# A hybrid attention layer: transfers of the dilated group on POOL's queue, a zero in SBUF for the first scans, and a set order on ACT and DVE at the start

## The chip, the cores and the metric

The kernel runs on one core of a Trainium2 chip. The engines are named as the profile names them: PE is TensorE (matmuls), DVE is VectorE, ACT is ScalarE, POOL is GpSimd, and SP is SyncE, which here only issues transfers (DMAs). Each engine takes its own instructions in order. SBUF is the on-chip memory, PSUM the banks into which PE writes. The metric is the time of one execution in microseconds (us).

## The reference

One layer of a decoder over x of 1024 tokens x 1024 channels, in float32. Eight heads of 64 use a dilated sliding window (group A), eight use stick-breaking attention (group B), and a gated feed-forward layer of 2816 follows:

```python
h = _rmsnorm(x, attn_norm_w[l])
proj = jnp.einsum('bsd,de->bse', h, w_in[l])          # qa ka va | qs ks vs, 512 columns each
qa = _apply_rope(_rmsnorm(heads(qa, 8), q_norm_w[l]), cos, sin)   # ka likewise
o_dil = _dilated_attention(qa, ka, heads(va, 8))      # branches merged by their denominators
o_sb = _stick_breaking(heads(qs, 8), heads(ksb, 8), heads(vs, 8))
mixed = concat(_rmsnorm(merge(o_dil), ...), _rmsnorm(merge(o_sb), ...))
x = x + mixed @ w_out[l]
h = _rmsnorm(x, ffn_norm_w[l])
x = x + (silu(h @ w_gate[l]) * (h @ w_up[l])) @ w_down[l]

# stick-breaking: beta[t,s] = sigmoid(q.k/8), for s < t
# A[t,s] = beta[t,s] * prod_{s<j<t} (1 - beta[t,j]);  o = A v
# dilated: branches with (window, dilation) (128,1), (512,4), (2048,16)
```

## The kernel before

**Numbers.** Every float32 operand is held as a high and a low part, and a product is three matmuls (lines 91, 94, 95). The high part is a copy on ACT, the low part a subtraction on DVE or POOL; for the tokens that is `split` (lines 61 and 62: hh and hl).

**Stages.** From 0 to about 75 us the eight token blocks of 128 are normed, turned over by PE (`norm_t`: xn on DVE at line 103, ptr at line 109, then `split`), and multiplied by the weights of group A's V (va). Then come the projections of K and Q, from about 165 us the dilated attention of four pairs of heads, from about 350 us the stick-breaking attention of four pairs, and then the output projection and the feed-forward layer. Projections of later pairs run in the background of the attention.

**What sets the order.** The kernel is written in the Tile framework. A scheduler orders each engine's instructions by a simulated time; tiles of one tag share a number of buffers, and `after(i, first, why)` tells the scheduler to put `i` behind `first` without a wait. All transfers are issued on SP's queue, in the order of the scheduler, and a transfer that waits for its data or its buffer holds those behind it.

**The start.** `tok_weights` (line 135) loads the weights of V in eight pieces (raw), makes the high part wt on ACT (line 146), and the low part wt on DVE for even pieces, on POOL for odd ones (line 147). `norm1` takes a token block's square on ACT (line 162); POOL makes the root of it (lines 56 and 57, rs).

**The dilated group.** For each half of a pair, `factors` writes row maxima and sums to memory (sums<-st, line 440, two transfers), reads them in another layout (x<-sums, line 442), weighs them on DVE and ACT (the first step is low<-x, line 448), writes the weights (fac<-fe, line 461) and reads them spread over the partitions (fac<-fac, line 466, two transfers). `finish` multiplies the branches by these on POOL (o, lines 594 and 595) and writes the sum to memory (oa<-o, line 596).

**The stick-breaking group.** K and Q of a pair come back from memory in pieces (rl<-raw, lines 288 and 291, three buffers); kh, kl, qs are their parts (lines 345, 346, 319, 320). For a block of 128 queries, PE computes scores (sc, lines 410 to 413), ACT takes two sigmoids, kp and pb (line 531), DVE a running product from the right over kp (line 534), and POOL (first head) or DVE (second head) multiplies pb by it (line 535). PE turns pb over (pt, line 551), ACT copies it (th), and PE multiplies by V (line 560). The scan's other operand is a column of zeros, which lies in a PSUM bank named aside; its tag "t" is also that of the dilated group's accumulator, so the bank is free when the last output of that group has been copied out:

```python
if aside[0] is None:                                   # attend_b, ahead of its first block
    aside[0] = PS.tile([128, 512], F32, "t", "aside")
    nc.vector.memset(aside[0][:, 0:1], 0.0)
```

Of the kernel before, what the change touches and what calls it, by code (L numbers as in the profile page):

```python
# [24 lines left out]
D = 1024  # L25
# [7 lines left out]
def f(ap):  # L33
    return ap.bitcast(F32)
# [3 lines left out]
def tile_hybrid_block(ctx, tc, x, attn_norm_w, w_in, q_norm_w, k_norm_w, dil_w, sb_w,  # L38
# [12 lines left out]
    mhalf = big.tile([128, 16], F32, name="mhalf")  # L51
    nc.vector.memset(mhalf, -0.5)
    def rstd_of(ss, n, pool, w):

        r = pool.tile([128, 16], F32, tag="rs", name="rs", bufs=6)
        nc.gpsimd.tensor_scalar(r[:, :w], ss, 1.0 / n, EPS, op0=ALU.mult, op1=ALU.add)
        nc.gpsimd.tensor_tensor(r[:, :w], r[:, :w], mhalf[:, :w], op=ALU.pow)
        return r

    def split(h, l, src):  # L60
        nc.scalar.activation(h, src, AF.Copy)  # L61
        nc.vector.tensor_tensor(l, src, f(h), op=ALU.subtract)  # L62

# [33 lines left out]
    def norm_t(xt, ss, wb, tb, dst, work, psum, tag, ptags, parts=1):  # L97

        r = rstd_of(ss, D, big, 1)
        xn = work(tag, "xn")  # L100
        for o in range(0, D, D // parts):
            cc = slice(o, o + D // parts)
            nc.vector.scalar_tensor_tensor(xn[:, cc], xt[:, cc], r[:, 0:1], wb[:, cc], op0=ALU.mult, op1=ALU.mult)
        hf, c = tb // 4, slice((tb % 4) * 128, (tb % 4) * 128 + 128)
        for g in range(2):
            pt = psum.tile([128, 512], F32, ptags[g], "ptr")
            for k in range(4):
                d = 4 * g + k
                nc.tensor.transpose(pt[:, k * 128:(k + 1) * 128], xn[:, d * 128:(d + 1) * 128], ident)
            pt = pt.rearrange("p (k t) -> p k t", k=4)  # L110
            for h, l, ks in dst(g, hf):
                if l is None:
                    if g:
                        nc.scalar.activation(h[:, :, c], pt[:, ks], AF.Copy)
                    else:
                        nc.vector.tensor_copy(h[:, :, c], pt[:, ks])
                else:
                    split(h[:, :, c], l[:, :, c], pt[:, ks])

# [16 lines left out]

    def tok_weights(col, tags):

        w = []
        for d in range(ND):  # L140
            if d % 2 == 0:
                w.append([att.tile([128, 2, 512], FR, tag=t, name="wt", bufs={"P": 6, "G": 2}.get(t, 4)) for t in tags[d:d + 2]])
            raw = big.tile([128, 512], F32, tag=("wraw", "wh", "wl")[d % 3], name="raw", bufs=3)
            nc.sync.dma_start(raw, w_in[d * 128:(d + 1) * 128, col:col + 512])
            h, l = (w[d // 2][k][:, d % 2, :] for k in range(2))
            nc.scalar.activation(h, raw, AF.Copy)
            (nc.gpsimd if col != 1024 or d % 2 else nc.vector).tensor_tensor(l, raw, f(h), op=ALU.subtract)
        return w

    for tb in range(NT):  # L150
# [3 lines left out]
        if tb == 0:  # L154
            nw = att.tile([128, D], F32, tag="v", name="nw", bufs=2)
            nc.sync.dma_start(nw, attn_norm_w.partition_broadcast(128))
            wv = tok_weights(1024, ("qs", "kh") * 4)

    def norm1(tb):
        ss = big.tile([128, 1], F32, tag="ss", name="ss", bufs=4)  # L160
        sq = P4("sq", "G")
        nc.scalar.activation(sq, xts[tb], AF.Square, accum_out=ss)
        norm_t(xts[tb], ss, nw, tb, lambda g, hf: [(hT[g][hf][0], hT[g][hf][1], slice(0, 4))], lambda tag, name: att.tile([128, D], F32, tag="kl", name=name, bufs=2), PS, "v", ("t", "pv"), 1 if tb else 2)

# [17 lines left out]
    for _ in range(12):  # L182
        nc.tensor.matmul(p[:, :128], ident, ident, start=True, stop=True)
    for tb in range(NT):
        norm1(tb)
        p = tok(wv, tb, "d")
# [248 lines left out]
    def factors(st):  # L435
# [5 lines left out]
        x = att.tile([128, 4, 2, 2, 2], F32, tag="x", name="x", bufs=2)  # L441
        nc.sync.dma_start(x.rearrange("p t l m s -> p t (l m s)"), sums.rearrange("(p t) l v -> p t (l v)", t=4))
        fac = dram.tile([2, 2, 512], F32, name="fac")
# [19 lines left out]
        def wide():  # L463
            t = P4("fac", "E").rearrange("p (l t) -> p l t", l=2)
            for s in range(2):
                nc.sync.dma_start(t[64 * s:64 * s + 64], fac[:, s].partition_broadcast(64))
            return t
# [58 lines left out]
    def unit_b(pr, s, qb, tag):  # L526
# [6 lines left out]
        rv = kp[:, n - 1::-1] if n == 1024 else kp[:, :n][:, ::-1]  # L533
        nc.vector.tensor_tensor_scan(rv, rv, aside[0][:, 0:1].to_broadcast([128, n]), 1.0, op0=ALU.mult, op1=ALU.bypass)  # L534
        (nc.gpsimd, nc.vector)[s].tensor_tensor(p[:, :n - 1], p[:, :n - 1], kp[:, 1:n], op=ALU.mult)
# [54 lines left out]
    def finish(pr, hf, o, wide):  # L590
# [4 lines left out]
        nc.gpsimd.tensor_tensor(t[0], t[0], t[1], op=ALU.add)  # L595
        nc.sync.dma_start(o[:, 512 * hf:512 * hf + 512], t[0])

# [26 lines left out]
    def attend_b(pr, o):  # L624

        if aside[0] is None:
            aside[0] = PS.tile([128, 512], F32, "t", "aside")
            nc.vector.memset(aside[0][:, 0:1], 0.0)
        late = None
        for g in range(4):  # L630
            pq = []
            for k in range(2):
# [536 lines left out]
```

## Time and profile before

| | |
|---|---|
| time, median of 3 runs | 1310.41 us (1310.36 to 1313.09) |
| profiled execution | 1310.01 us |
| its span | 1308.2 us, 18283 instructions |
| PE busy | 1264.8 us, 97% of the span |
| weight loads (beside PE) | 998.6 us, 76% |
| DVE busy | 839.7 us, 64% |
| ACT busy | 621.4 us, 47% |
| POOL busy | 390.3 us, 30% |
| mean granted clock of PE | 0.99 |
| transfers | all on one queue, 171.42 MB, 42.1% of the 16 DMA engines |

The span reaches from the first to the last instruction in the trace. In a timeline, the number in brackets is how long the engine stood idle before the instruction, with what released it; several like instructions in a row are one line with their count, and then the time is that of all together. SPq is SP's queue, and the time there is the time to issue the transfer, not to land it. The clock is the share of full speed that was granted to PE.

### The profile page before, as it was taken

How to read it: one execution, taken by the hardware profiler on the slowest of the kernel's cores; microseconds unless marked ns; L12 is line 12 of the kernel's file. 1: busy time of each engine (PE TensorE's matmuls, PEld its weight loads, DVE VectorE, ACT ScalarE, POOL GpSimd, SP SyncE). 2: the span in 40 equal slices, each digit the busy share in tenths (PEclk: the TensorE clock that was granted, in tenths of full speed). 3: DMA queues.
4: the chain of work that ended last, by engine and by line, in shares of the span. 5: the costliest groups of instructions: out<-in, count | busy, mean ns of one | idle time of the engine just before them, and what ended most of it. 6: DMA issues, size and time to landing. Idle time of an engine off the chain costs nothing.

```text
span 1308.2 us, 18283 instructions
## 1 busy us (share of the span) xinstructions
PE 1264.8 (97%) x6260; PEld 998.6 (76%) x6260; DVE 839.7 (64%) x1408; ACT 621.4 (47%) x1305; POOL 390.3 (30%) x334
## 2 busy tenths in 40 slices
PE   7999999999879988999999999999999999999998
PEld 6888887776656766767888888888888887788786
DVE  4224346566477768664788676665546878986775
ACT  6331177776587777753565222233333223344443
POOL 6378722422223234243312222221222321100000
PEclk9999999999989999999999999999999999999999
DMA  9533143544513243132236545323456448503642
GB/s 286 209 112 106 57 130 99 132 132 131 137 60 113 65 170 137 42 103 91 73 123 224 169 153 166 103 87 101 133 150 196 127 151 304 165 18 109 197 137 81
DMA packets 189325, 172.59 MB, mean 132 GB/s; under 512 B 33712, under 2 KB 134192, under 8 KB 189232
## 3 DMA queue, kind: packets, MB, share of 16 engines
q1 hardware_dynamic: 189232, 171.42, 42.1%
q8 instruction: 49, 0.80, 0.3%
q14 instruction: 44, 0.36, 0.1%
HBM read 133.96 MB, written 37.42 MB: 131 GB/s over the span
## 4 chain that ended last, share of the span: by engine, by line
PE 87%; DMA 4%; ACT 3%; DVE 3%; issue 2%; SPq 0%; POOL 0%; DVEq 0%; ACTq 0%; POOLq 0%
PE yd L1069 14%; PE gu L94 11%; PE gu L95 11%; PE gu L91 11%; PE va L95 3%; PE va L91 3%; PE va L94 3%; PE pp L91 3%; PE pp L94 3%; PE pp L95 3%; PE pv L560 2%; PE yo L91 2%; PE pv L487 2%; PE yo L95 2%; PE yo L94 2%; PE pt L551 2%
## 5 line engine op out<-in xcount | busy, mean ns | idle before, releaser
L843 ACT ACTIVATE wh<-wr 128x512 fp32r<-128x512 f32 x132 | 83.4, 632 | 209.5 <-PE gu L94 164.2
L94 PE MATMUL gu<-t,wh 128*128 128x512 f32 x352 | 139.0, 395 | 0.0
L91 PE MATMUL gu<-t,wh 128*128 128x512 f32 x352 | 138.9, 395 | 0.0
L95 PE MATMUL gu<-t,wl 128*128 128x512 f32 x352 | 138.9, 394 | 0.0
L1069 PE MATMUL yd<-dl,dh 128*128 128x512 f32 x308 | 122.1, 396 | 3.1 <-DVE dl L844 3.1
L1069 PE MATMUL yd<-dh,dl 128*128 128x512 f32 x308 | 121.2, 393 | 0.0
L94 PE MATMUL gu<-b,wh 128*128 128x512 f32 x264 | 104.5, 396 | 0.0
L91 PE MATMUL gu<-b,wh 128*128 128x512 f32 x264 | 104.4, 396 | 0.0
L95 PE MATMUL gu<-b,wl 128*128 128x512 f32 x264 | 104.2, 396 | 0.0
L534 DVE TENSOR_TENSOR_SCAN kp<-kp,aside 128x128 f32<-128x128 f32 (+7 forms) x64 | 85.4, 1347 | 29.2 <-ACT kp L531 28.9
L844 DVE TENSOR_TENSOR wl<-wr,wh 128x512 fp32r<-128x512 f32 x105 | 80.5, 767 | 7.6 <-ACT wh L843 7.5
L1069 PE MATMUL yd<-dh 128*128 128x512 f32 x308 | 84.6, 395 | 0.0
L91 PE MATMUL va<-wt,hh 128*128 128x512 f32 x192 | 76.6, 405 | 2.9 <-ACT hh L61 2.9
L95 PE MATMUL va<-wt,hl 128*128 128x512 f32 x192 | 76.5, 401 | 1.9 <-DVE hl L62 1.9
L91 PEld LDWEIGHTS gu<-t,wh 128*128 128x128 f32 x352 | 66.2, 188 | 15.7
L94 PEld LDWEIGHTS gu<-t,wh 128*128 128x128 f32 x352 | 66.2, 188 | 15.7
L95 PEld LDWEIGHTS gu<-t,wl 128*128 128x128 f32 x352 | 66.2, 188 | 15.6
L91 PE MATMUL pp<-hh,wh 128*128 128x512 f32 x192 | 77.9, 406 | 0.0
L843 ACT ACTIVATE dh<-wd 128x512 fp32r<-128x512 f32 x55 | 34.8, 632 | 90.0 <-PE yd L1069 82.4
L94 PE MATMUL va<-wt,hh 128*128 128x512 f32 x192 | 76.3, 400 | 0.0
L95 PE MATMUL pp<-hh,wl 128*128 128x512 f32 x192 | 76.0, 396 | 0.0
L94 PE MATMUL pp<-hl,wh 128*128 128x512 f32 x192 | 75.6, 394 | 0.0
(214 smaller groups left out, 3067.7 us busy)
## 6 DMA issues: line engine op xcount, KB each, us to landing
wd<-in_w_down_dram SPq DMA_DIRECT2D x88, 256.0 KB, 2.9
wr<-in_w_gate_dram SPq DMA_DIRECT2D x80, 256.0 KB, 3.0
wr<-in_w_up_dram SPq DMA_DIRECT2D x60, 256.0 KB, 3.1
raw<-in_w_in_dram SPq DMA_DIRECT2D x48, 256.0 KB, 4.2
raw<-in_w_out_dram SPq DMA_DIRECT2D x32, 256.0 KB, 2.9
raw<-rq SPq DMA_DIRECT2D x24, 256.0 KB, 2.7
g<-gu SPq DMA_DIRECT2D x20, 256.0 KB, 5.4
xt<-in_x_dram SPq DMA_DIRECT2D x8, 512.0 KB, 6.9
```

The lines of the kernel that those rows point to most:

```text
L91: i = nc.tensor.matmul(ps, a[0], b[0], start=first, stop=False)
L94: nc.tensor.matmul(ps, a[0], b[1], start=False, stop=False)
L95: return nc.tensor.matmul(ps, a[1], b[0], start=False, stop=last)
L487: nc.tensor.matmul(pr.acc[lay][64 * s:64 * s + 64, cols], v[:, 64 * s:64 * s + 64], th[:, c:c + n], start=first, stop=last)
L534: nc.vector.tensor_tensor_scan(rv, rv, aside[0][:, 0:1].to_broadcast([128, n]), 1.0, op0=ALU.mult, op1=ALU.bypass)
L551: i = nc.tensor.transpose(pt[:, c:c + 128], pq[k][s][:, j * 128:(j + 1) * 128], ident)
L560: i = nc.tensor.matmul(pr.pv[64 * s:64 * s + 64, c - n:c], pr.v[:, j, 64 * s:64 * s + 64], th[:, n * s:n * s + n], start=j == 0, stop=j == ...
L843: nc.scalar.activation(h, r, AF.Copy)
L844: two(n).tensor_tensor(l, r, f(h), op=ALU.subtract)
L1069: mm = nc.tensor.matmul(pp[k], a[x][:, c], b[y], start=not more and j == 0 and x + y == 0, stop=j == HF - 1 and x == 1, skip_group_check=True)
```

## The change

Three things are changed.

1. The order at the start. All eight raw pieces of V's weights are asked for ahead, as before, but their low parts are all made on DVE. `after` sets this order on ACT (k = 0) and on DVE (k = 1): weight pieces 0 and 1, both parts of token block 0, weight pieces 2 to 7. The square of token block 1 is set between pieces 4 and 5, and those of later blocks behind the first high part of the block two before.
2. In the dilated group, x<-sums, fac<-fac (two) and oa<-o are issued on POOL's queue instead of SP's, 32 transfers in all.
3. A column of zeros, `zero`, lies in SBUF from the start. The scans of the first four query blocks of the first stick-breaking pair (128 to 512 columns, two heads) use it; the bank aside is taken only ahead of the fifth block (g == 2).

```diff
+    zero = big.tile([128, 1], F32, name="zero")
+    nc.vector.memset(zero, 0.0)
...
     def split(h, l, src):
-        nc.scalar.activation(h, src, AF.Copy)
-        nc.vector.tensor_tensor(l, src, f(h), op=ALU.subtract)
+        i = nc.scalar.activation(h, src, AF.Copy)
+        return i, nc.vector.tensor_tensor(l, src, f(h), op=ALU.subtract)
...
-    def tok_weights(col, tags):
-
-        w = []
+    def tok_raw(col, d):
+        raw = big.tile([128, 512], F32, tag=("wraw", "wh", "wl")[d % 3], name="raw", bufs=3)
+        nc.sync.dma_start(raw, w_in[d * 128:(d + 1) * 128, col:col + 512])
+        return raw
+
+    def tok_weights(col, tags, raws=None):
+
+        w, parts = [], []
         for d in range(ND):
...
-            raw = big.tile([128, 512], F32, tag=("wraw", "wh", "wl")[d % 3], name="raw", bufs=3)
-            nc.sync.dma_start(raw, w_in[d * 128:(d + 1) * 128, col:col + 512])
+            raw = raws[d] if raws else tok_raw(col, d)
             h, l = (w[d // 2][k][:, d % 2, :] for k in range(2))
-            nc.scalar.activation(h, raw, AF.Copy)
-            (nc.gpsimd if col != 1024 or d % 2 else nc.vector).tensor_tensor(l, raw, f(h), op=ALU.subtract)
-        return w
+            i = nc.scalar.activation(h, raw, AF.Copy)
+            parts.append((i, (nc.vector if raws else nc.gpsimd).tensor_tensor(l, raw, f(h), op=ALU.subtract)))
+        return (w, parts) if raws else w
...
-            wv = tok_weights(1024, ("qs", "kh") * 4)
+            wv, wparts = tok_weights(1024, ("qs", "kh") * 4, [tok_raw(1024, d) for d in range(ND)])
...
+    before = []
     for tb in range(NT):
-        norm1(tb)
+        sq, made = norm1(tb)
+        if tb == 0:
+
+            for k in range(2):
+                after(made[0][k], wparts[1][k], "order of the first products")
+                after(wparts[2][k], made[1][k], "order of the first products")
+                for d in range(3, ND):
+                    after(wparts[d][k], wparts[d - 1][k], "order of the first products")
+        if tb == 1:
+            after(sq, wparts[4][0], "order of the first products")
+            after(wparts[5][0], sq, "order of the first products")
+        if tb > 1:
+            after(sq, before[-2][1][0], "order of the first products")
+        before.append(made)
...
         x = att.tile([128, 4, 2, 2, 2], F32, tag="x", name="x", bufs=2)
-        nc.sync.dma_start(x.rearrange("p t l m s -> p t (l m s)"), sums.rearrange("(p t) l v -> p t (l v)", t=4))
+        nc.gpsimd.dma_start(x.rearrange("p t l m s -> p t (l m s)"), sums.rearrange("(p t) l v -> p t (l v)", t=4))
...
-                nc.sync.dma_start(t[64 * s:64 * s + 64], fac[:, s].partition_broadcast(64))
+                nc.gpsimd.dma_start(t[64 * s:64 * s + 64], fac[:, s].partition_broadcast(64))
...
-        nc.vector.tensor_tensor_scan(rv, rv, aside[0][:, 0:1].to_broadcast([128, n]), 1.0, op0=ALU.mult, op1=ALU.bypass)
+        nc.vector.tensor_tensor_scan(rv, rv, (aside[0] if aside[0] is not None else zero)[:, 0:1].to_broadcast([128, n]), 1.0, op0=ALU.mult, op1=ALU.bypass)
...
-        nc.sync.dma_start(o[:, 512 * hf:512 * hf + 512], t[0])
+        nc.gpsimd.dma_start(o[:, 512 * hf:512 * hf + 512], t[0])
...
     def attend_b(pr, o):
 
-        if aside[0] is None:
-            aside[0] = PS.tile([128, 512], F32, "t", "aside")
-            nc.vector.memset(aside[0][:, 0:1], 0.0)
         late = None
         for g in range(4):
+            if aside[0] is None and g == 2:
+                aside[0] = PS.tile([128, 512], F32, "t", "aside")
+                nc.vector.memset(aside[0][:, 0:1], 0.0)
```

The change moves instructions in the scheduler's order. DVE's order at the start, in the kernel before (wt is a weight's low part, xn a normed token block, of block 0 in two halves, hl the tokens' low parts):

```order
L103 SCALAR_TENSOR_TENSOR xn<-xt,rs,nw 128x512 x2
L147 TENSOR_TENSOR wt<-raw,wt 128x512 x3
L62 TENSOR_TENSOR hl<-ptr,hh 128x4x128 x2
L147 TENSOR_TENSOR wt<-raw,wt 128x512
L103 SCALAR_TENSOR_TENSOR xn<-xt,rs,nw 128x1024 x3
L62 TENSOR_TENSOR hl<-ptr,hh 128x4x128 x2
```

Here three xn stand between the last weight piece on DVE and the next hl. In the changed kernel DVE starts with:

```order
L106 SCALAR_TENSOR_TENSOR xn<-xt,rs,nw 128x512 x2
L155 TENSOR_TENSOR wt<-raw,wt 128x512 x2
L64 TENSOR_TENSOR hl<-ptr,hh 128x4x128 x2
L155 TENSOR_TENSOR wt<-raw,wt 128x512 x4
L106 SCALAR_TENSOR_TENSOR xn<-xt,rs,nw 128x1024
L155 TENSOR_TENSOR wt<-raw,wt 128x512 x2
L106 SCALAR_TENSOR_TENSOR xn<-xt,rs,nw 128x1024
L64 TENSOR_TENSOR hl<-ptr,hh 128x4x128 x2
```

The low parts of block 0 stand behind two weight pieces instead of three, all eight pieces are in the list, and ahead of the next hl there is one xn less, with two weight pieces between.

SP's order at the passage to the stick-breaking group, before (o<-oa and nw belong to later stages; rl 64x512 are halves of a K piece, rl 128x512 Q pieces):

```order
L291 DMA rl<-raw_1940 64x512 x2
L596 DMA oa_144<-o 128x512
L440 DMA sums<-st 128x4x4
L660 DMA o<-oa_142 128x512
L800 DMA nw<-in_ffn_norm_w_dram 128x1024
L291 DMA rl<-raw_1940 64x512 x2
L440 DMA sums<-st 512x1x4
L288 DMA rl<-raw_2237 128x512 x2
L442 DMA x<-sums 128x32
```

Here oa<-o is ahead of the sums and of the rest of K. SP's order at the same place, changed:

```order
L313 DMA rl<-raw_1942 64x512 x2
L462 DMA sums<-st 128x4x4
L682 DMA o<-oa_144 128x512
L822 DMA nw<-in_ffn_norm_w_dram 128x1024
L313 DMA rl<-raw_1942 64x512 x2
L462 DMA sums<-st 512x1x4
L310 DMA rl<-raw_2239 128x512 x2
```

oa<-o is gone from the head of this piece and x<-sums from its end; what remains keeps its order.

DVE's order at the same place, before (th is a copied turn of the dilated group, SCALAR_TENSOR_TENSOR of kp the scan):

```order
L431 ISA st 128x1
L346 TENSOR_TENSOR kl<-rl,kh 64x512 x3
L517 COPY th<-pt 128x512
L346 TENSOR_TENSOR kl<-rl,kh 64x512
L517 COPY th<-pt 128x512
L320 TENSOR_TENSOR qs<-rl,qs 64x512 x4
L628 MEMSET aside 128x1
L534 SCALAR_TENSOR_TENSOR kp<-kp,aside 128x128 x2
```

Here all scans stand behind the memset of the bank, and that behind four qs. DVE's order there, changed:

```order
L368 TENSOR_TENSOR kl<-rl,kh 64x512 x3
L556 SCALAR_TENSOR_TENSOR kp<-kp,zero 128x128
L539 COPY th<-pt 128x512
L556 SCALAR_TENSOR_TENSOR kp<-kp,zero 128x128
L557 TENSOR_TENSOR pb<-pb,kp 128x127
L368 TENSOR_TENSOR kl<-rl,kh 64x512
L556 SCALAR_TENSOR_TENSOR kp<-kp,zero 128x256
L539 COPY th<-pt 128x512
L342 TENSOR_TENSOR qs<-rl,qs 64x512 x2
L556 SCALAR_TENSOR_TENSOR kp<-kp,zero 128x256
L342 TENSOR_TENSOR qs<-rl,qs 64x512
L557 TENSOR_TENSOR pb<-pb,kp 128x255
```

The scans of 128 columns stand ahead of the fourth kl, those of 256 among the qs, and the memset of the bank between the scans of 384.

## Rows read from the trace of the kernel before

**Rows 1.** Page part 4, the chain that ended last, by engine.

```profile
PE 87%; DMA 4%; ACT 3%; DVE 3%; issue 2%; SPq 0%; POOL 0%; DVEq 0%; ACTq 0%; POOLq 0%
```

**Rows 2.** Windows: stretch, length, busy of five engines, TensorE clock, DMA share, GB/s.

```profile
10.00:15.00 5.00, 2.71 (x7) 1.89 (x8) 4.83 (x5) 4.61 (x10) 4.74 (x5) 0.83 1.04 408
15.00:20.00 5.00, 5.00 (x20) 3.94 (x20) 2.86 (x3) 2.14 (x4) 4.54 (x6) 0.83 1.08 358
25.00:300.00 275.00, 275.00 (x1522) 218.39 (x1522) 123.14 (x372) 136.22 (x351) 135.02 (x124) 1.00 0.43 127
360.00:370.00 10.00, 5.40 (x24) 3.92 (x25) 7.79 (x14) 7.29 (x18) 2.31 (x3) 0.50 0.28 84
```

**Rows 3.** Timeline, start: start us, us, engine line operation out<-in count [idle before].

```profile
8.16 0.69 DVE L147 TENSOR_TENSOR wt<-raw,wt 128x512 fp32r<-128x512 f32 x1
8.87 5.87 POOL L147 TENSOR_TENSOR wt<-raw,wt 128x512 fp32r<-128x512 f32 x4 [2.30 <-ACT wt L146]
...
11.36 0.50 PE L91 MATMUL va<-wt,hh 128*128 128x512 f32 x1 [2.58 <-ACT hh L61]
...
13.02 0.61 PE L95 MATMUL va<-wt,hl 128*128 128x512 f32 x1 [0.92 <-DVE hl L62]
...
13.48 1.81 DVE L147 TENSOR_TENSOR wt<-raw,wt 128x512 fp32r<-128x512 f32 x1
...
13.50 1.06 ACT L162 ACTIVATE sq<-xt 128x1024 f32<-128x1024 f32 x1
...
20.94 1.28 DVE L103 SCALAR_TENSOR_TENSOR xn<-xt,rs,nw 128x1024 f32<-128x1024 f32 x1 [1.65 <-DMA wbq<-in_q_norm_w_dram]
...
22.14 1.28 DVE L62 TENSOR_TENSOR hl<-ptr,hh 128x512 fp32r<-128x512 f32 x2
...
22.88 0.50 PE L95 MATMUL va<-wt,hl 128*128 128x512 f32 x1 [1.01 <-DVE hl L62]
```

**Rows 4.** What SP's queue waited for: us in total, times, longest us.

```profile
SPq L596 <- POOL o L595: 20.5, 6, 4.5
SPq L442 <- DMA sums<-st: 20.1, 8, 4.1
```

**Rows 5.** Timeline at 305 to 311 us, and at 396.

```profile
305.81 1.03 SPq L288 DMA_DIRECT2D rl<-raw  x2
...
310.66 0.63 ACT L319 ACTIVATE qs<-rl 64x512 fp32r<-64x512 f32 x1 [2.27 <-DMA rl<-raw]
...
396.56 0.60 SPq L466 DMA_DIRECT2D fac<-fac  x1
```

**Rows 6.** Timeline, the passage between the two groups of heads.

```profile
348.48 3.67 DVE L346 TENSOR_TENSOR kl<-rl,kh 64x512 fp32r<-64x512 f32 x3
...
349.27 1.61 POOL L595 TENSOR_TENSOR o<-o 128x512 f32<-128x512 f32 x1
...
350.91 0.33 SPq L596 DMA_DIRECT2D oa<-o  x1
...
352.89 1.09 SPq L291 DMA_DIRECT2D rl<-raw  x2
...
359.74 0.63 ACT L345 ACTIVATE kh<-rl 128x512 fp32r<-128x512 f32 x1 [6.26 <-DMA rl<-raw]
...
360.90 2.08 PE L487 MATMUL pv<-th,v 128*64 128x256 f32 x12 [4.96 <-ACT th L515]
...
364.19 2.05 DVE L320 TENSOR_TENSOR qs<-rl,qs 64x512 fp32r<-64x512 f32 x2 [0.94 <-ACT qs L319]
...
366.34 0.73 DVE L534 TENSOR_TENSOR_SCAN kp<-kp,aside 128x128 f32<-128x128 f32 x2
...
367.30 0.47 PE L551 MATMUL pt<-ident,pb 128*128 128x128 f32 x1 [3.49 <-POOL pb L535]
```

**Rows 7.** All transfers of line 442: ns min/median/max of the issue, and landing.

```profile
L442 SPq DMA_DIRECT2D x<-sums x8: 319/332/409, 196.7 to 359.9; - x8
...
DMA to landing us min/median/max: 1.5/1.8/3.2
```

More of the change, by code (lines that the diff above doesn't have):

```diff
@@ L99, in norm_t @@
         r = rstd_of(ss, D, big, 1)
+        made = []
         xn = work(tag, "xn")
@@ L117, in norm_t @@
                 else:
-                    split(h[:, :, c], l[:, :, c], pt[:, ks])
+                    made.append(split(h[:, :, c], l[:, :, c], pt[:, ks]))
+        return made
     att_ctx = ExitStack()
@@ L161, in norm1 @@
         sq = P4("sq", "G")
-        nc.scalar.activation(sq, xts[tb], AF.Square, accum_out=ss)
-        norm_t(xts[tb], ss, nw, tb, lambda g, hf: [(hT[g][hf][0], hT[g][hf][1], slice(0, 4))], lambda tag, name: att.tile([128, D], F32, tag="kl", name=name, bufs=2), PS, "v", ("t", "pv"), 1 if tb else 2)
+        i = nc.scalar.activation(sq, xts[tb], AF.Square, accum_out=ss)
+        return i, norm_t(xts[tb], ss, nw, tb, lambda g, hf: [(hT[g][hf][0], hT[g][hf][1], slice(0, 4))], lambda tag, name: att.tile([128, D], F32, tag="kl", name=name, bufs=2), PS, "v", ("t", "pv"), 1 if tb else 2)
     dram = att_ctx.enter_context(tc.tile_pool(name="dram", bufs=1, space=bass.MemoryType.DRAM))
```

## The prediction

> **What bounds the kernel now.** I read the chain of waits first: TensorE (PE) holds 87% of it [rows 1]. Next, the windows: from 25 to 300 us PE is busy 275.00 of 275.00 us, whatever the other engines wait for there [rows 2]. So an edit can change the time only where PE is idle or runs below its full clock. The diff touches three such places: the start, a spot near 306 to 315 us, and the passage from the dilated to the stick-breaking group. There PE is busy 5.40 of the 10 us from 360 to 370, at a granted clock of 0.50, the lower of its two levels, 1.2 GHz [rows 2]. I then read the timelines there, and last the waits of SyncE's (SP's) queue.
>
> The profiled execution took 1310.01 us: 1308.2 of span and 1.8 around it. The median of the runs is 1310.41, so a sum made against 1310.0 stands for the median too, to within 0.4.
>
> **1. The order at the start.** PE starts the V products at 11.36, 2.58 us late for the hh of ACT, and its third waits 0.92 for the hl of DVE at 13.02 [rows 3]. PE loses its last time to DVE at 22.88: the hl of token block 1 comes at 22.14, behind an xn of block 3 at 20.94, which had itself stood 1.65 us [rows 3]. In the new order only two xn and two wt stand between the square of block 1 and those hl. The sum by hand: xt of block 1 is there at 13.50 as before, when its square starts [rows 3]. The square and POOL's two small steps give the xn from about 15.9 to 17.2 (1.28 as in the row at 20.94), two wt of 0.69 to 18.5, the next xn to 19.8, the first hl (0.64, half of the 1.28 for two) to 20.45 [rows 3]. That is 22.88 - 20.45 = 2.4 us earlier, and PE never waits again before 300. Block 0 is not late for it: its last matmul comes at about 19, since the eight low parts on DVE alone go at 0.69, while beside POOL's four (5.87) they took up to 1.81 [rows 3].
>
> What can go back is clock. From 10 to 20 us the granted clock is 0.83 [rows 2], which is a third of the time at the lower level: 3.3 us, costing half, 1.7. Before, this fell on the stretch that had slack behind it, as block 1 was later than block 0. Now block 0's end and block 1's hl are close, so some of it shows. I take **-1.5**, between -0.3 and -2.4.
>
> **2. Thirty-two transfers from SP's queue to POOL's.** SP stood 20.5 us in six waits before oa<-o and 20.1 in eight before x<-sums [rows 4]. Most of that is hidden by a PE that is full. It shows where a load behind the waiting one is what PE lacks.
>
> At 303 to 311 us the q pieces (rl, issued 305.81) let ACT wait 2.27 for qs at 310.66 [rows 5]. Ahead of them stood oa<-o, but the K pieces before them also need the first kl, so little is won: -0.3. At 396.56 two fac<-fac, 0.60 us each, stand on SP ahead of four rl [rows 5]; I take -0.3 of the 1.2, as those rl come one for one behind kl afterwards. Together **-0.6** (0 to -2).
>
> At the passage oa<-o waits for POOL's o, 349.27 + 1.61 = 350.88, and goes out at 350.91; the fourth K piece follows at 352.89 [rows 6]. Without it SP could issue that piece when its slot is free, after the first of the three kl: 348.48 + 3.67/3 = 349.7. That is 3.1 us earlier, and if the landing takes as long, ACT's kh moves from 359.74 to about 356.6, and with it the th for which PE waits 4.96 until 360.90 [rows 6]. What stands behind kh on ACT and DVE moves along.
>
> **3. The zero in SBUF.** Today the first scans stand behind the bank "aside" at 366.34, behind four qs; POOL's pb and then PE (3.49 idle until 367.30) wait for them [rows 6]. With a zero in SBUF the 128-column scans run in DVE's gap before kl. This takes their 0.73 out of the stretch after kh, and with kp before qs on ACT also the 0.94 that DVE waits there at 364.19 [rows 6]. Next late is then DVE itself, which has the same kl, th, qs and larger scans to do after kh; so the 3.49 don't come off whole. The passage moves by 3.1 + 0.73 + 0.94 = 4.8.
>
> Against this stands that the scan now has both inputs in SBUF. The nearest row is the wt on DVE: 0.69 alone, 1.81 beside POOL's wt [rows 3], and the three kl of 3.67 under POOL's o, 1.22 each [rows 6]. Eight scans meet four pb and an acc of POOL; in the dearest case each of five meetings costs 1.81 - 0.69 = 1.1, but not all are late: I take +1.0, of 0 to 3. The passage gives **-3.8** (-1 to -7; the far end includes PE's half clock from 360 to 370, of which up to 2.7 us, half of 5.40, can come back if the pause gets short).
>
> The Trainium skill, "SBUF — State Buffer", section "Who interferes with whom", speaks against this edit: a VectorE operation with two SBUF inputs and a GpSimd operation that reads SBUF exclude each other, and the later one blocks. The two rows agree with it, 0.69 against 1.81; if it never bit here, the sum would be 1.0 us lower.
>
> **4. What POOL pays.** No transfer of before is on POOL's queue, so its price is bounded. From below: SP's own issue, 0.33 us for x<-sums [rows 7]; from above, a 128x512 operation of POOL, 5.87/4 = 1.47 [rows 3]. For 32 that is 11 to 47 us on POOL. Behind the waits on POOL stand its qf, wl, o and pb. The first three are needed late, and PE is full over them. The one engine that follows closely is DVE, whose in-order minimum reads x; x lands 1.8 us after issue [rows 7]. Six x of the dilated group may come up to 1.47 - 0.33 = 1.1 later, at most 6.8 us on DVE; PE's fullness from 25 to 300 [rows 2] covers four of them. I take **+0.8**, of 0 to 3. The nearest row is SP's own, as the transfers are small.
>
> **Sum:** -1.5 - 0.6 - 3.8 + 0.8 = -5.1, so 1310.0 - 5.1 = 1304.9, say **1305.0**. All behind the passage keeps its order, so what is won stays.
>
> **The rivals.**
>
> A. The loads are late for the transfer, not for SP. The fourth K piece takes from 352.89 to 359.74 [rows 6]; if it is held by the traffic around it, issuing it 3.1 us earlier gives nothing, nor do the 0.6. What remains is -1.5, scans and ACT wait of 0.73 + 0.94 less 1.0, and 0.8: 1310.0 - 1.4 = 1308.6. For: 6.9 us to land is long. Against: SP demonstrably stands before it. The Trainium skill, "DMA: Bandwidth & Descriptors", section "Issuing engines are not separate DMA queues", says that the issuer saves only sequencer time, since the same DMA engines do the work. By that rule A decides; the trace bears it out only where SP does not stand, and here it stands.
>
> B. The gap moves on: DVE and ACT, not loads, set the first stick-breaking blocks, and of the 3.8 only about 1 is kept: -1.5 - 0.6 - 1 + 0.8 = -2.3, 1307.7. For: DVE is busy 7.79 and ACT 7.29 of 10 us from 360 to 370 [rows 2]. Against: part of that work starts earlier in the new order.
>
> C. The start gives nothing, as PE's clock takes back all 1.5: 1306.5.
>
> D. Slower, by one mechanism: POOL's queue holds x. A transfer from POOL that comes 2.6 us later than one from SP would delay DVE's minimum six times, 6 x 2.6 = 15.6, and if PE followed, the 5.9 won would become +9.7, 1319.7; with a third of that covered, 1314.5. It decides from 1.0 us per x (5.9/6) with no cover. Against it: PE's full 275 us, in which kl of 3.67 for three on DVE cost nothing. A rule of the skill's same SBUF page fits: transfers that GpSimd issues can be starved by VectorE; no row here shows one, and the price of D does not use it.
>
> That the change doesn't do what it says is part of A: the order shows the scans ahead of the bank and oa<-o gone from SP, so only the effect is open.
>
> **How the numbers follow.** Forecast 0.55 (own range 1301 to 1307.5), A 0.16, B 0.13, C 0.08, D 0.08. Below 1301 lies the passage with the clock back, 1310.0 - 2.4 - 2 - 7 = 1298.6; the range goes from 1298.5 to 1311, which holds A, B and C with the +3 of POOL or of the scans, and leaves out D and the far tails. A measurement of this kernel can tell about 0.2%, 2.6 us: faster means below 1307.8. The forecast gives 0.54 of its 0.55, C 0.08, B half, A a fifth: 0.72. Same: the rest of A, B and the forecast, 0.20. Slower: D, 0.08.
>
> **What would show it.** Right: the third V product of block 1 at about 20.5; the fourth K piece issued near 350, kh near 356.5; scans of 128 columns before kl, with no pause of PE before pt; PE's times from 380 on earlier by 4 to 6 us, and constant to the end. Wrong: x landing over 2.8 us after its issue on POOL with DVE standing at the minimum; PE pauses between 190 and 350; a scan on zero of twice the length of one on the bank; a fourth K piece that is issued early and lands at 359.

## The result, and the profile after

The changed kernel takes 1303.67 us (median; 1303.33 to 1307.06), the kernel before 1310.41: a ratio of 0.9944, with a 95% interval of 0.9928 to 0.9960, so 6.7 us less. 1305.0 was forecast, in a range of 1298.5 to 1311. One execution of an experiment below (oa_only) took 2968.52 us, more than twice all others, and is left out of its median.

The page of the changed kernel. First PE's line (busy us, share of the span, instructions), then the new queue of the 32 transfers, with packets, MB and share of the engines:

```profile
PE 1264.6 (97%) x6260; PEld 997.8 (77%) x6260; DVE 844.3 (65%) x1413; ACT 620.6 (48%) x1305; POOL 404.5 (31%) x362
...
q0 software_dynamic: 2176, 6.42, 1.8%
```

PE's busy time is the same within 0.2 us (1264.8 before); the span fell from 1308.2 to 1301.9. So it is pauses and slow stretches that went, not work. The windows answer to [rows 2]:

```profile
15.00:20.00 5.00, 4.41 (x15) 3.43 (x16) 4.55 (x6) 3.63 (x7) 1.66 (x3) 0.70 1.07 357
25.00:300.00 275.00, 273.99 (x1515) 216.99 (x1514) 124.75 (x372) 138.77 (x357) 148.32 (x148) 1.00 0.43 127
360.00:370.00 10.00, 8.80 (x42) 6.53 (x42) 8.62 (x11) 6.97 (x18) 3.19 (x2) 0.83 0.25 80
```

From 360 to 370 us PE is busy 8.80 us at a clock of 0.83 (before 5.40 at 0.50). From 25 to 300, where it was full, it now stands 1.0 us. From 15 to 20 the clock is 0.70, lower than before.

How far ahead PE is can be read as the start of one and the same instruction in both traces. The table takes copies on ACT that follow PE, and DVE's last sum (at their times before, in us), and gives how much earlier they start after the change:

| at, before | 193.3 | 235.8 | 299.4 | 316.7 | 341.2 | 373.9 | 591.8 | last sum, 1302.4 |
|---|---|---|---|---|---|---|---|---|
| ahead | 1.7 | 1.8 | 0.6 | 2.2 | 2.2 | 7.7 | 9.2 | 6.3 |

So the start gave 1.7 us, 1.2 were lost between 236 and 299, 1.6 won at 306 to 315, 5.5 in the passage, 1.5 in the stick-breaking group, and 2.8 lost in the down projection, most of it near 1085 us.

**The start.** The timeline, as in [rows 3]:

```profile
13.31 1.06 ACT L170 ACTIVATE sq<-xt 128x1024 f32<-128x1024 f32 x1 [1.95 <-DMA xt<-in_x_dram]
...
15.03 0.49 PE L93 MATMUL va<-wt,hh 128*128 128x512 f32 x1 [1.48 <-ACT wt L154]
...
17.05 1.94 PE L112 MATMUL ptr<-ident,xn 128*128 128x128 f32 x8 [0.32 <-DVE xn L106]
...
18.64 0.78 PE L96 MATMUL va<-wt,hh 128*128 128x512 f32 x1
...
21.16 0.39 PE L97 MATMUL va<-wt,hl 128*128 128x512 f32 x1
```

PE waits for the sixth weight piece at 15.03 (1.48 us), which stands on ACT behind the square at 13.31. The tokens' turn then goes from 17.05, ahead of the last five products of block 0, and block 1's third product starts at 21.16 instead of 22.88. The half-speed stretch is seen in the product at 18.64: 0.78 us, where 0.40 is usual.

**The loss at 245 us.** The same view, 237 to 248 us:

```profile
237.28 2.53 POOL L616 TENSOR_TENSOR o<-o,fac 128x512 f32<-128x512 f32 x2 [6.82 <-DMA fac<-fac]
...
239.78 1.27 POOL L76 TENSOR_TENSOR wl<-raw,wh 128x512 fp32r<-128x512 f32 x1
...
240.99 0.61 POOL L464 DMA_DIRECT2D x<-sums  x1
...
244.27 0.32 DVE L470 TENSOR_TENSOR low<-x 128x8 f32<-128x8 f32 x1 [2.54 <-DMA x<-sums]
...
246.49 0.66 PE L509 MATMUL pv<-th,vc 128*64 128x128 f32 x8 [1.01 <-ACT th L537]
```

POOL multiplies (o<-o,fac), makes a weight's low part, and only then issues x<-sums, at 240.99. x lands 3.3 us later; DVE stands 2.54 us before its minimum (low), and 2 us later PE stands 1.01. The list of transfers (count, size, median us from issue to landing) has x<-sums at 3.0, which from SP was 1.8 [rows 7]:

```profile
oa<-o POOLq DMA_DIRECT2D x8, 256.0 KB, 3.4
...
x<-sums POOLq DMA_DIRECT2D x8, 16.0 KB, 3.0
```

**The passage.** The same view, answering to [rows 6]:

```profile
346.28 4.05 DVE L368 TENSOR_TENSOR kl<-rl,kh 64x512 fp32r<-64x512 f32 x3
...
347.94 1.09 SPq L313 DMA_DIRECT2D rl<-raw  x2
...
350.36 0.42 DVE L556 TENSOR_TENSOR_SCAN kp<-kp,zero 128x128 f32<-128x128 f32 x1
...
353.76 0.63 ACT L367 ACTIVATE kh<-rl 128x512 fp32r<-128x512 f32 x1 [1.94 <-DMA rl<-raw]
...
355.60 0.65 PE L509 MATMUL pv<-th,v 128*64 128x256 f32 x4
...
361.07 0.44 PE L573 MATMUL pt<-ident,pb 128*128 128x128 f32 x2 [2.07 <-DVE pb L557]
...
362.90 1.36 POOL L557 TENSOR_TENSOR pb<-pb,kp 128x383 f32<-128x383 f32 x1 [5.05 <-DVE aside L652]
```

The fourth K piece is issued at 347.94 instead of 352.89, kh starts at 353.76 instead of 359.74, the first scan at 350.36 instead of 366.34, ahead of the fourth kl; of each difference 2.2 us is the lead that PE had already. PE goes into pv at 355.60 without a wait; the 4.96 and the 3.49 are gone. New are smaller waits, of which the largest is 2.07 at 361.07 for a pb that stands on DVE behind qs. POOL's pb of 383 elements at 362.90, beside a scan, takes 1.36 us.

### The profile page after: what moved, and what is told of

Read it like the earlier page. It is cut to its first block, busy times and chain, and to the rows that moved or that the text cites. A ratio compares the mean times of both kernels' runs of the same rounds, so it can differ in the third digit from the quotient of the medians.

```text
span 1301.9 us, 18289 instructions
## 1 busy us (share of the span) xinstructions
PE 1264.6 (97%) x6260; PEld 997.8 (77%) x6260; DVE 844.3 (65%) x1413; ACT 620.6 (48%) x1305; POOL 404.5 (31%) x362
## 4 chain that ended last, share of the span: by engine, by line
PE 61%; ACT 3%; DVE 3%; DMA 2%; issue 2%; DVEq 0%; SPq 0%; POOL 0%; ACTq 0%; POOLq 0%
PE yd L1091 14%; PE gu L96 11%; PE gu L97 11%; PE gu L93 11%; PE yo L93 2%; PE yo L97 2%; PE yo L96 2%; PE pv L582 2%; PE pt L573 2%; PE sc L432 1%; DMA wd<-in_w_down_dram 1%; PE pp L93 1%; PE pp L96 1%; PE pp L97 1%; PE sc L433 1%
## 5 line engine op out<-in xcount | busy, mean ns | idle before, releaser
L556 DVE TENSOR_TENSOR_SCAN kp<-kp,aside 128x640 f32<-128x640 f32 (+7 forms) x56 | 79.3, 1426 | 27.8 <-ACT kp L553 27.6
L866 POOL TENSOR_TENSOR wl<-wr,wh 128x512 fp32r<-128x512 f32 x27 | 38.1, 1411 | 124.9 <-ACT wh L865 99.0
L557 POOL TENSOR_TENSOR pb<-pb,kp 128x127 f32<-128x127 f32 (+7 forms) x32 | 40.2, 1257 | 116.4 <-DVE kp L556 53.8
```

The lines of the kernel that those rows point to most:

```text
L556: nc.vector.tensor_tensor_scan(rv, rv, (aside[0] if aside[0] is not None else zero)[:, 0:1].to_broadcast([128, n]), 1.0, op0=ALU.mult, op1 ...
L866: two(n).tensor_tensor(l, r, f(h), op=ALU.subtract)
```

## The experiments

In the sets of the experiments, the kernel before took 1312.7 to 1313.8 us (medians; single executions from 1309.2 to 1316.7), so a kernel is compared with the one before, or the changed one, of its own set, and stretches are compared by the lead of its trace over the trace of before. Such a lead sets one execution against one other: that of before took 1310.01 us, about 3 us less than the medians just given, that of queue_only is the longest of its ten (1318.11, median 1312.80), and that of zero_only the shortest (1308.37, median 1312.57). So a lead shows where time is won, and the times have to show how much. All leads, in us:

| kernel | 193 | 236 | 299 | 317 | 341 | 374 | 592 | last |
|---|---|---|---|---|---|---|---|---|
| changed, first | 1.7 | 1.8 | 0.6 | 2.2 | 2.2 | 7.7 | 9.2 | 6.3 |
| after_again | 2.0 | 2.0 | -0.2 | 0.5 | 0.5 | 6.0 | 3.9 | 4.0 |
| after_third | 1.9 | 1.8 | -2.5 | -2.0 | -3.1 | 2.2 | -0.5 | -0.2 |
| start_only | 2.7 | 2.7 | 2.7 | 2.1 | 2.1 | 2.2 | -0.9 | -0.5 |
| queue_only | 1.2 | -0.1 | -6.4 | -5.5 | -5.5 | -1.1 | -5.4 | -8.0 |
| zero_only | 0.0 | 0.0 | 0.1 | -0.1 | -0.1 | 2.6 | 1.1 | 1.5 |
| queue_zero | -0.3 | -0.6 | -6.5 | -5.1 | -6.0 | 0.6 | -1.0 | -1.3 |
| x_back | 2.5 | 2.5 | 1.6 | 3.3 | 2.7 | 8.9 | 8.2 | 6.1 |
| x_back_again | 2.4 | 2.4 | 1.8 | 3.5 | 3.5 | 9.3 | 9.5 | 10.4 |
| oa_only | 2.6 | 2.6 | 2.7 | 3.6 | 1.9 | 7.6 | 8.0 | 8.3 |
| all_zero | 2.6 | 2.5 | -2.0 | -0.9 | -0.9 | 4.9 | -8.7 | -8.5 |
| sq_late | 1.5 | 1.2 | -4.5 | -3.2 | -3.2 | 2.0 | 1.9 | 2.1 |
| sq_late_x | 1.4 | 1.4 | 0.6 | 0.9 | 0.0 | 5.6 | 3.6 | 3.3 |

**start_only**: the changed kernel with

```diff
-        nc.gpsimd.dma_start(x.rearrange(...), sums.rearrange(...))
+        nc.sync.dma_start(x.rearrange(...), sums.rearrange(...))
...
-            if aside[0] is None and g == 2:
+        if aside[0] is None:
```

and the same for fac<-fac and oa<-o.

> Only the order at the start (all low parts of V's weights on DVE, the order of weights and tokens); transfers on SP and scans on the bank as before. The changed kernel's trace is 1.75 us ahead from 28 us on. Theory (what is won at a place where PE waited stays): PE 1.7 to 1.8 us ahead up to 340 us, passage unchanged, 1308.6 us (1308.0 to 1309.2). Rival (later waits absorb it: the passage waits for transfers, not for PE): still ahead at 340, but the time within 0.5 us of 1310.4.

Measured: 1310.34 against 1312.69 of the set, a ratio of 0.9982 (0.9969 to 0.9994), so 2.4 us less. The lead is 2.7 us at 193 and still 2.2 at 374, with the passage unchanged; that is the theory, a little more than expected. In this one trace it melts from 2.2 to -0.9 in the stick-breaking group, which the median of the times doesn't show. Its clock from 15 to 20 us, in the view of the windows, explains why 2.7 and not 1.75:

```profile
15.00:20.00 5.00, 3.88 (x19) 2.55 (x18) 4.56 (x6) 4.35 (x10) 1.65 (x5) 1.00 1.07 356
```

1.00, where the three traces of the changed kernel have 0.70, 0.70 and 0.71, with the same order of instructions. The traces with 1.00 there and this order (start_only, x_back, x_back_again, oa_only, all_zero) lead by 2.4 to 2.7 us at 193, the three with 0.70 by 1.7 to 2.0: the lower level takes 0.4 to 1.0 us. The start of before depends on the clock as well: queue_only, which leaves the start as it was, keeps 1.00 where before has 0.83 [rows 2], and leads by 1.2 us at 193:

```profile
10.00:20.00 10.00, 7.73 (x34) 5.59 (x34) 7.66 (x8) 8.33 (x16) 9.09 (x9) 1.00 1.06 381
```

So with like clocks the new order is worth 1.2 to 1.5 us where both stay at 1.00, and 1.7 to 2.0 where both fall.

**queue_only**: the kernel before with the three nc.sync.dma_start of x<-sums, fac<-fac and oa<-o made nc.gpsimd.dma_start.

> Only the 32 transfers on POOL's queue; start and scans as before. Theory: the fourth K piece is issued 3 us earlier, kh at the passage comes 3 us earlier, and the wait of PE before pv shrinks by as much; the wait before pt (3.5 us) stays, as the scans stay behind the bank; about 1 us is lost where x lands late (at 245 us): 1310.4 - 3 - 0.5 + 1 = 1307.9 (1307 to 1309). Rival A (the piece is held by the transfer): kh no earlier, 1310.4 to 1311.5.

Measured: 1312.80 against 1312.69, 0.9988 (0.9974 to 1.0002): no gain. Neither theory as it stands. In the passage the kernel does win what was expected and more, 4.3 us (from -5.5 to -1.1). The timeline there:

```profile
354.88 1.09 SPq L291 DMA_DIRECT2D rl<-raw  x2
...
361.04 0.63 ACT L345 ACTIVATE kh<-rl 128x512 fp32r<-128x512 f32 x1 [1.26 <-DMA rl<-raw]
...
368.60 0.48 PE L551 MATMUL pt<-ident,pb 128*128 128x128 f32 x1 [4.66 <-POOL pb L535]
```

Before, issue and kh were at 352.89 and 359.74; less the 5.5 that this trace is late, they are at 349.4 and 355.6 here, 3.5 and 4.2 us earlier. That speaks against rival A. The wait before pt stays, 4.66 us, as the scans are still behind the bank. But in this trace more than that is spent before, most of it at 245 us:

```profile
241.55 2.52 POOL L594 TENSOR_TENSOR o<-o,fac 128x512 f32<-128x512 f32 x2 [8.16 <-DMA fac<-fac]
...
245.25 0.60 POOL L442 DMA_DIRECT2D x<-sums  x1
...
248.69 0.17 DVE L448 TENSOR_TENSOR low<-x 128x8 f32<-128x8 f32 x1 [5.06 <-DMA x<-sums]
```

x is issued at 245.25, behind o<-o,fac which began at 241.55, and DVE stands 5.06 us. The windows of that stretch show what follows:

```profile
245.00:250.00 5.00, 2.43 (x16) 1.58 (x14) 1.25 (x4) 0.03 (x1) 4.79 (x6) 0.97 0.51 161
250.00:255.00 5.00, 4.27 (x18) 3.45 (x19) 2.24 (x14) 3.82 (x12) 0.00 (x0) 0.50 0.21 56
```

PE is busy 2.43 of 5 us, and in the next five its clock is 0.50, the lower level: 6.2 us are lost from 236 to 299, though PE's waits there come to 3.3. Another wait of 1.00 stands at 225 us, behind the x before, for which DVE stood 3.19.

**zero_only**: the kernel before with the zero and the later bank.

> Only the zero in SBUF for the first eight scans; transfers on SP, start as before. Theory: kh at the passage stays at 359.7, PE's wait of 5 us before pv stays, the one of 3.5 us before pt goes, some of it returns before the next scans: 1308.4 (1307.5 to 1309.5). Rival (scans with two SBUF inputs are held by POOL, or DVE is the bound there): 1310 or more.

Measured: 1312.57 against 1312.69, 0.9995 (0.9979 to 1.0011); in the passage 2.7 us are won (from -0.1 to 2.6). The timeline there:

```profile
352.64 1.09 SPq L293 DMA_DIRECT2D rl<-raw  x2
...
358.99 0.63 ACT L347 ACTIVATE kh<-rl 128x512 fp32r<-128x512 f32 x1 [5.22 <-DMA rl<-raw]
...
360.22 0.44 PE L412 MATMUL sc<-kh,qs 128*128 128x384 f32 x1 [4.14 <-ACT pb L533]
...
364.99 0.44 PE L412 MATMUL sc<-kh,qs 128*128 128x384 f32 x1 [0.83 <-ACT pb L533]
...
367.64 0.61 PE L553 MATMUL pt<-ident,pb 128*128 128x128 f32 x2 [1.10 <-DVE pb L537]
```

The wait of 4.96 is now 4.14, before the next scores and not before pv, since kh still comes at 358.99; the one of 3.49 has become 0.83 and 1.10. Alone this is worth 2.7 us at the place, a little over what was expected; of the 2 us that were expected in the time (1308.4 against 1310.4) nothing is to be seen.

**queue_zero**: both, without the order at the start.

> The transfers on POOL's queue and the zero, without the order at the start. Theory (the parts add): 1303.7 + 1.75 = 1305.4 (1304.8 to 1306). If the two parts at the passage need each other, queue_only and zero_only together win less than this does: the sum of their gains against the gain here tells it. Rival: the start's gain is absorbed later, and this run is within 0.5 us of 1303.7.

Measured: 1308.29 against 1312.69, 0.9965 (0.9948 to 0.9982), 4.4 us less; 5 were expected. In the passage it wins 6.6 (-6.0 to 0.6), near 4.3 + 2.7: by the traces the two add there. By the times, which the expectation set as the test, they don't: alone the two parts win nothing (1312.80 and 1312.57 against 1312.69), together 4.4. As single executions of these three kernels spread over 8 to 11 us, this isn't settled. With the 2.4 of start_only the 4.4 make 6.8, near what the whole change wins. At 245 us queue_zero loses 5.9.

**after_again** and **after_third**: the changed kernel, unchanged.

> The changed kernel itself again, beside the others of this set: how far its trace differs from one execution to another. Theory: x, issued on POOL behind its multiplications, lands late at 245 us by an amount that differs between executions (1.2 us lost in its first trace, 6.5 us with the queue alone), so PE's lead from 240 to 300 us lies between +0.6 and -5, the rest of the trace alike; time 6 to 7 us below the kernel before.

> The changed kernel a third time, beside the next three. Theory: DVE stands 2.5 to 5 us for x at 245 us and PE's lead falls by 1 to 6 us there; in the passage PE wins 5.4 to 5.5 us, as in its first two traces; time 1303 to 1307, 6 to 8 us below the kernel before.

Measured: 1305.24 against 1313.78 (0.9933; 0.9912 to 0.9955), and 1304.04 against 1312.81 (0.9943; 0.9924 to 0.9961). DVE stands 3.60 and 4.15 us for x at 245, and 2.2 and 4.3 us of lead go from 236 to 299; in the passage 5.5 and 5.3 are won. The times are 8.5 and 8.8 us below the kernel before, more than the 6 to 8 expected. The executions of after_third reach from 1301 to 1310, and the traced one, in which the 4.3 were lost, took 1310.17.

**x_back** and **x_back_again**: the changed kernel with one line undone.

```diff
-        nc.gpsimd.dma_start(x.rearrange("p t l m s -> p t (l m s)"), ...)
+        nc.sync.dma_start(x.rearrange("p t l m s -> p t (l m s)"), ...)
```

> The changed kernel with x<-sums issued on SP's queue again; fac<-fac and oa<-o stay on POOL's, start and zero as changed. The engines' orders apart from SP and POOL are those of the changed kernel. Theory (POOL's queue holds x, which holds DVE, which holds PE at 245 us): PE keeps its lead of 1.75 us through 240 to 300 us, and the time is 1 to 4 us below the changed kernel's of the same set. Rival (x back on SP holds SP's loads as before): the fourth K piece at the passage late again or the q pieces near 306 us, and the time the changed kernel's or 1 to 3 us above it.

> The changed kernel with x<-sums on SP again, a second time, for a firmer number: theory 1.5 to 3 us below the changed kernel of the same set, no wait of DVE for x at 245 us; rival (the first comparison, 1.9 us on four executions each, was chance): within 1 us of it.

Measured: 1303.35 and 1302.42, where the changed kernel has 1305.24 and 1304.04 in the same sets; against before 0.9917 (0.9902 to 0.9932) and 0.9931 (0.9909 to 0.9953). The 10 executions average 1302.6, the 14 of the changed kernel 1305.0: 2.3 us, with a standard error of 1.2 from their spread of 2.6 and 3.1. DVE no longer waits for x at 245:

```profile
240.88 0.23 DVE L470 TENSOR_TENSOR low<-x 128x8 f32<-128x8 f32 x1
...
242.71 2.67 DVE L478 TENSOR_TENSOR fd<-fe,x 128x8 f32<-128x8 f32 x1 [0.28 <-ACT fe L476]
```

The minimum at 240.88 starts without a wait. Of the lead 0.5 to 0.9 us still go here; in this trace the two fd behind it take 2.75 us (the first 2.67), where they take 0.26 in the changed kernel; they stand beside two qf of POOL, which run from 243.20 to 245.35. Passage and q pieces are won as before, so the rival falls. That the wait at 245 us goes is shown; that the time falls by 2.3 us below the changed kernel's is at the edge of what this spread can tell.

**oa_only**: x_back, with fac<-fac on SP as well.

> Start and zero as changed; of the transfers only oa<-o on POOL's queue, x<-sums and fac<-fac on SP's. Theory (the one wait on SP that mattered was oa<-o's, ahead of the fourth K piece): passage as won as with all three, 5.5 to 6.5 us, no wait for x at 245 us, time within 1 us of x_back_again. Rival (fac<-fac on SP holds the loads behind it as before): 1 us or more of the gain missing at 306 or 396 us, and the time 1 to 3 us above x_back_again.

Measured: 1304.68 (five executions) against 1302.42 of x_back_again and 1304.04 of the changed kernel; 0.9937 of before (0.9917 to 0.9956). No lead is lost at 245 (2.6 to 2.7), and the passage wins 5.7. But at 305 us, where x_back's lead goes from 1.6 to 3.3, the lead here falls from 2.7 to 1.9. The 3.6 of the table at 317 is no measure of it: the copy follows products that stand earlier in PE's order in this kernel, and the same products of PE lead by 1.9 from 315 on. The timeline there:

```profile
299.01 5.38 DVE L368 TENSOR_TENSOR kl<-rl,kh 64x512 fp32r<-64x512 f32 x3
...
304.87 0.30 PE L451 MATMUL sc<-kh,qf 128*128 128x128 f32 x1 [2.20 <-DVE st L453]
```

Three kl take 5.38 us on DVE (4.06 in x_back), PE stands 2.20 us for the st behind them, and from 305 to 310 its clock is 0.66. The theory holds for the passage, which moving oa<-o alone wins. At 306 us the gain is missing, as the rival has it, but not for the rival's reason: the loads are in time, and the qs at 307.06 starts without a wait. By its time the kernel is 2.3 us above x_back_again, within the spread. It isn't settled.

**all_zero**: the changed kernel with `g == 2` out of reach, so that all 64 scans read the zero in SBUF.

```diff
-            if aside[0] is None and g == 2:
+            if aside[0] is None and g == 9:
```

> The changed kernel with all 64 scans on the zero in SBUF, the bank never taken. This gives 56 more scans two inputs in SBUF. Theory (such a scan and POOL's multiplication hold each other): POOL's pb of 512 columns or more get longer (means of 1.32 us at 640 and 2.00 at 1024 columns in the changed kernel) by a fifth or more where they meet a scan, and the time rises by 2 to 10 us. Rival (no such hold; what is longer at the first eight is chance): the means of scans and pb within 3%, and the time within 1 us of the changed kernel's.

Measured: 1318.27 against 1305.24 of after_again, 13 us more, and 1.0033 (1.0020 to 1.0045) of before. The lead goes from 4.9 at 374 to -8.7 at 592. Two lines of the groups by line and shape (count, busy us, mean ns), of the changed kernel:

```profile
L556 DVE TENSOR_TENSOR_SCAN kp<-kp,aside 128x1024 f32<-128x1024 f32 x8 | 18.2, 2278 | 1.3 <-ACT kp L553 1.2
...
L556 DVE TENSOR_TENSOR_SCAN kp<-kp,aside 128x768 f32<-128x768 f32 x8 | 14.0, 1754 | 6.0 <-ACT kp L553 6.0
```

and of all_zero:

```profile
L556 DVE TENSOR_TENSOR_SCAN kp<-kp,zero 128x1024 f32<-128x1024 f32 x8 | 26.5, 3314 | 0.1
...
L556 DVE TENSOR_TENSOR_SCAN kp<-kp,zero 128x768 f32<-128x768 f32 x8 | 18.1, 2266 | 5.4 <-ACT kp L553 5.3
```

Scans of 1024 go from 2278 to 3314 ns, of 768 from 1754 to 2266. Two of the scans of 1024 show what makes them longer:

```profile
393.96 2.27 DVE L556 TENSOR_TENSOR_SCAN kp<-kp,zero 128x1024 f32<-128x1024 f32 x1
...
396.99 3.98 DVE L556 TENSOR_TENSOR_SCAN kp<-kp,zero 128x1024 f32<-128x1024 f32 x1
```

The first, with no operation of POOL beside it, is as long as one on the bank; the second runs beside POOL's pb (396.40, 2.42 us) and o<-o,fac (398.78, 3.28 us). In the changed kernel a scan on the bank beside the same o<-o,fac keeps its 2.29 us, at 394.85. So the hold is real and dearer than I expected, and it falls on DVE, the engine that scans, more than on POOL: there pb of 1024 columns go from 2.00 to 2.33 us in the mean, and those of 640 to 896 stay as they were. The theory had the hold, but its price on the wrong engine, and the 13 us lie above its 2 to 10. The Trainium skill, "SBUF — State Buffer", section "Who interferes with whom", says that a VectorE operation with two SBUF inputs and a GpSimd operation that reads SBUF exclude each other; this trace agrees, with the scan's column of zeros as the second input.

**sq_late** and **sq_late_x**: the square of token block 1 behind the last weight piece, the second with x on SP.

```diff
-            after(sq, wparts[4][0], "order of the first products")
-            after(wparts[5][0], sq, "order of the first products")
+            after(sq, wparts[7][0], "order of the first products")
```

> The changed kernel with the square of token block 1 set behind all eight weight pieces on ACT, not between the fifth and the sixth. In the changed kernel ACT stands 1.95 us before that square, with three pieces behind it, and PE stands 1.48 us for the sixth piece. Theory: ACT makes the last three pieces while it would stand (3 x 0.56 = 1.7 us), block 0 ends near 15 instead of 21 us, the square starts as early as before, and PE is 1 to 2 us further ahead from 30 us on. Rival (the pause of PE before block 1's tokens lowers its clock, and that takes the gain): within 0.5 us of the changed kernel's lead of 1.75.

> x<-sums on SP, and the square of token block 1 behind all eight weight pieces. With x on POOL this start was 0.8 to 1.7 us further ahead at 28 us than the changed one, but PE then stood 1.6 us for hl before 80 us. Theory: the same again, a lead of 3.2 to 3.6 us at 28 us and of 1 to 2 at 165, so 0.5 to 1 us slower than x_back_again. Rival (the later loss was the one execution's): 0.5 to 1.5 us faster than x_back_again.

Measured: 1308.30 against 1305.24 of after_again, and 1306.27 against 1302.42 of x_back_again: 3 to 4 us more. The start itself does as the theory has it:

```profile
10.17 3.23 ACT L154 ACTIVATE wt<-raw 128x512 fp32r<-128x512 f32 x6
...
13.30 1.05 ACT L170 ACTIVATE sq<-xt 128x1024 f32<-128x1024 f32 x1
...
19.39 0.51 PE L97 MATMUL va<-wt,hl 128*128 128x512 f32 x1 [0.46 <-DVE hl L64]
```

ACT makes six weight pieces from 10.17 in 3.23 us and the square starts at 13.30, as early as in the changed kernel; block 1's third product is at 19.39. At 29 us the lead is 3.5 (1.8 in the changed kernel). At 193 it is 1.5 and 1.4. The scheduler, given the other order, also moved the xn and hl of later blocks, and PE stands 1.6 us for an hl at 34.24. The gain of the start is lost again with that: at 193 the two are 0.5 and 1.0 us behind after_again and x_back_again. The rest of the 3 to 4 us wasn't followed; in the trace of sq_late 5.6 of lead go from 236 to 299, against 2.2 in after_again. The passage wins 5.2 and 5.6.

## Why the prediction was right

The time and the sign came as forecast, 1.3 us from it, but the terms differ, some against each other, and that the sum came so close is in part luck: in the first trace the passage, the small places and the stick-breaking group won 4.2 us more than was forecast, and a loss of 2.8 in the down projection, which was not forecast, took most of that back.

- **Start, -1.5 forecast.** -1.7 in the first trace, -2.0 and -1.9 in the others. The clock took part of it, as the term had it (2.4 to 2.7 where it stays at 1.00), but not all, so rival C falls. The step was right: in start_only, with the clock at 1.00, the last product of block 0 starts at 18.57 and the third of block 1 at 20.17, as forecast (about 19 and 20.5); at the lower level they start at 20.45 and 21.16. What the sum lacked is the wait for the sixth weight piece, 1.5 us in both.
- **Small places, -0.6 forecast.** -1.6, -0.7 and -0.4 at 306 to 315 us in the three traces of the changed kernel, and little at 396. The q pieces gained more from SP's freedom than the 0.3 that I read from kl; start_only and zero_only, with x and oa on SP, lose 0.6 and 0.2 there.
- **Passage, -3.8 forecast, -1 to -7.** -5.5, -5.5 and -5.3, inside the bounds, more than taken. The reasons were as told: issue 3.5 (3.1 forecast, where the rows give 3.2) and kh 4.2 earlier and 4.3 us won through the queue alone, 2.7 through the zero alone, and in the traces they nearly add (6.6 together), which the times leave open. A part of the clock came back as at the far end of the bound: 0.83 instead of 0.50. Rival A falls by queue_only, rival B by the 5.3 to 5.5 themselves. From 374 to 592 us the lead grows by 1.5 in the first trace and falls by 2.1 and 2.7 in the others; start_only, which won nothing in the passage, loses 3.1 there, so such a loss needs no win that is given back; what makes it stays open.
- **The hold of zero and POOL, +1.0 inside that term.** For the first eight it is small: POOL's pb of 383 took 1.36 beside a scan, 0.86 before, and that of 511 took 1.83, 1.09 before. all_zero shows the price where the scans are long.
- **POOL's queue, +0.8 forecast, 0 to 3.** This is the term that was mis-sized: +1.2, +2.2 and +4.3 in the changed kernel's traces, 6.2 and 5.9 with the queue but not the start. The step that failed is "The nearest row is SP's own, as the transfers are small". The price isn't the issue (0.61 us) and only in part the landing (3.0 against 1.8): x stands on POOL behind multiplications, which wait for fac. That is rival D, but DVE stood for x six times (5.4 us in all in the first trace) and PE followed at one of them, in after_third with the clock behind it; my point of 1.0 us per x spread over six what happens at one. x_back takes it away. I overlooked that fac itself lands later from POOL's queue there. The two fac ahead of these multiplications, before and then changed:

```profile
L466 SPq DMA_DIRECT2D fac<-fac x2: 601/606/611, 230.6 to 231.3; - x2
DMA to landing us min/median/max: 4.4/4.7/4.9
...
L488 POOL DMA_DIRECT2D fac<-fac x2: 598/603/608, 229.3 to 229.9; - x2
DMA to landing us min/median/max: 5.6/6.4/7.2
```

The later of the two lands 7.2 to 8.6 us after its issue in the ten traces that have it on POOL, and 4.5 to 5.0 in the four that have it on SP. No run puts fac alone back on SP, so whether x would then be in time from POOL's queue is untested.

- **"What is won stays."** Not in the first trace: of 9.2 us 2.8 are lost, at the first block of the down projection.

```profile
1075.27 1.35 DVE L1072 TENSOR_TENSOR lk<-g 128x512 f32<-128x512 f32 x2 [1.42 <-DMA g<-gu]
...
1088.49 0.58 PE L1091 MATMUL yd<-dl,dh 128*128 128x512 f32 x1 [2.31 <-DVE dl L866]
```

DVE waits 1.42 for g there, PE 2.31 for dl. The wait of 2.3 is in the trace of before too, but after the change PE's clock is 0.88 from 1085 to 1090 and 0.78 from 1090 to 1095, before 1.00, and there is another pause of 0.49: 0.6 + 1.1 + 0.5 = 2.2 us. In after_again and after_third no lead is lost from 592 us to the end (3.9 to 4.0, -0.5 to -0.2), while x_back loses 2.1 and queue_only 2.6. So it belongs to an execution, not to the change; what decides when the clock falls there stays open. Added up, the start, the small places, the passage and the loss at 245 us give 7.6 us in the first trace, 6.0 and 3.3 in the other two; the times give 6.7, 8.5 and 8.8.

## What to carry to other kernels

Look for the one wait on a queue that stands ahead of a load which the bounding engine lacks; oa<-o was such a wait, and most of the others on SP, 20 us for x among them, cost nothing that these runs show. A transfer that waits takes its place at the head of the line along to the new queue: move it only if nothing is late behind or ahead of it there, look at how late each transfer lands from the new queue (fac here), and leave a small transfer that an in-order engine reads at once, such as x, on the queue that issues it earliest. An operand that is moved from PSUM to SBUF for an earlier start can be worth it for a few short operations and cost 13 us for all.

## What the runs showed of the hardware

A pause of PE costs more than its length when the clock falls behind it: from 236 to 299 us, waits of 3.3 us became a loss of 6.2 in queue_only, with 0.50 in the five us from 250, and waits of 2.5 a loss of 4.3 in after_third, while after 1.0 us of pause in the first trace of the changed kernel and 1.9 in after_again the clock stayed at 1.00.

The same program with the same order from 0 to 20 us had a clock of 0.70 in three traces, and kernels with the same instructions there (start_only, x_back, oa_only) 1.00, with pauses of PE of like length, 1.48 and 1.51 us. In the same way the start of before had 0.83 from 10 to 20 us, and in queue_only 1.00. I have no reason for that.

A scan over 1024 columns with a column of zeros in SBUF took 3314 ns on average, 2278 with the column in PSUM; with nothing of POOL beside it, the one with SBUF took 2.27 us too. The issue of x or oa held POOL 0.59 us in the median, SP 0.33; that of fac took 0.6 us on either. From POOL's queue x landed 1.2 us later in the median (3.0 against 1.8), oa 1.3 (3.4 against 2.1) and fac 0.7 (4.7 against 4.0), but at 230 us by 2.2 us and more.
